# Soft mixture of experts on one core: SP's queue reordered between two products, and the part sums of one weight set begun a stage later

## The chip, the cores and the metric

The kernel runs on one core of one Trainium2 chip. The metric is the device time of one execution in microseconds (us), lower is better; times of several executions are given by their median. The engines are TensorE (PE in the profile, its weight loads PEld), VectorE (DVE), ScalarE (ACT), GpSimd (POOL) and SyncE (SP). SP, ACT and POOL also issue the transfers (DMAs) between the chip's memory and the core.

## The reference

Eight experts, every token goes to all of them, weighted by a softmax over its router logits. Inputs are x (16 x 512 x 512), router_logits (16 x 512 x 8) and expert_weights (8 x 512 x 2048), all float32.

```python
probs = softmax(router_logits)                 # over the 8 experts
output = zeros(16, 512, 2048)
for e in range(8):
    output += probs[:, :, e:e+1] * (x @ expert_weights[e])
```

Written as one product, each token has a row of 8 x 512 entries (x times the probability of each expert), which is multiplied by a matrix of 4096 x 2048.

## The kernel before

The one large product is split as in Strassen's scheme, so that fewer multiplications are needed and sums take their place. On the outermost level there are seven products, P1 to P7, over halves of tokens, experts and columns; each works on a left operand (tokens times probabilities, z tiles, made by VectorE) and a right operand (a sum of weight blocks, w tiles). Every product is done for 16 blocks q of tokens, and inside of it the same scheme is used again: seven inner steps, in the order 1, 5, 6, 2, 7, 3, 4, each of eight matmuls of 512 columns into a PSUM bank. Some stages go a level deeper still.

The work stands in a list of stages. A stage holds one or two products and takes the inner steps of the two in turn, so a stage with two has 14 places, called slots (0 to 13). After a step, its result is copied out of the bank by ScalarE or added by VectorE (the function post). P5 and P6 share stages: k5 = 15 holds P5 of blocks 0 and 1, stage 16 P6 of block 0 alone, stages 17 to 30 hold P6 of block q and P5 of block q + 1, and k6 = 31 holds P6 of block 15. P7 and P4 begin at k7 = 32, and P3 at k3 = 48.

Three things set the order of the work around the steps:

- Hooks. `at(stage, slot, make)` says that make is called ahead of the step in that slot. Loads, fetches of weights and the queueing of sums all hang on such hooks. `slots_after` moves a place on by a number of slots, across stages.
- VectorE's queue. `later(cost, make)` puts a sum into a queue; with a last argument of True at its front. The program takes from it by a plain reckoning of how far TensorE and VectorE are. `flush(task)` takes from it until a given task is done. What comes out of this is a fixed order of instructions for VectorE.
- The queues of SP, ACT and POOL. Each issues its transfers in the order in which the program calls them, and an instruction at the head of a queue waits there for its semaphores. ACT's queue holds both its copies out of the banks and its fetches of weights.

After each step, run(stage) also calls three sets of loads, by n, the number of steps done:

```python
                if n == 5:
                    store_loads(stage + 1)
                if n == 7:
                    finish_loads(stage + 2)
```

finish_loads issues two DMA transposes on SP, which turn a block of x that POOL has loaded and cast (tile xs) into tile xT. store_loads stores the transposed block to memory (x) for later products. Both go through SP's queue.

SP's queue in stages 15 to 31 also carries: the four base fetches of P6 (function fetch_at: the parts of P1 that were kept in memory, h tiles), from which VectorE subtracts P5's results (joined); two stores of each left operand of P6 (keep_z); the loads of x and of the probabilities for the stage after next; and in four places an early part of P3's left operand (the table EARLY: stages k5 + 5, + 8, + 11, + 12). This early part is made in tile u, of which there is a single buffer, by early_make, and stored by SP to operand3.

P4's weights are made from the second half of the weights (loaded anew, block 21) less sums called t2, and from these the inner sums. by_parts does this in four parts, 38 slots apart, each in one w tile:

```python
    by_parts(k5 + 2, 4, 38, 4, load_p4, less_t2, (9, 20))
```

A part loads four blocks by POOL (at the given stage and slot), subtracts t2 from three of them 9 slots later and stores these (less_t2), and queues four inner sums 20 slots after the load, each of which is stored by POOL as soon as it is made (sums_in_place; the DRAM tiles are called wd). w tiles come from a pool of 15 buffers. The first part loads at stage 17, slot 4; the last at stage 25, slot 6, and its sums are queued at stage 26, slot 12.

In stage k6 - 3 = 28, begin_ahead (slot 1) fetches a block of the weights of P7 (t3) into a new w tile, and ahead_part (slots 2 and 13) fetches parts of it into tile u, all on ACT's queue. turnover fetches P4's finished weights from stage k6 on.

Of the kernel before, what the change touches and what calls it, by code (L numbers as in the profile page):

```python
# [31 lines left out]
def kernel(  # L32
# [68 lines left out]
    def note(i):  # L101
        last[i.ins.engine] = i.ins
        if ordered[0]:
            tc.keep_in_program_order(i)
# [18 lines left out]
    def sp(o, i):  # L123
        note(nc.sync.dma_start(out=o, in_=i))

    def pool(o, i, **how):
        note(nc.gpsimd.dma_start(out=o, in_=i, **how))  # L127
# [12 lines left out]
    def new_w():  # L140
        return wpool.tile([P, K8, NB], f16, name="w", tag="w")

    def new_u():
        return zpool.tile([P, K8, HQ], f16, name="u", tag="u", bufs=1)
# [223 lines left out]
    class Task:  # L368
# [5 lines left out]
        def run(self):  # L374
            self.done = True
            clock["dve"] += self.cost
            self.make()

    def flush(task):
        while task is not None and not task.done:  # L380
            queue.popleft().run()
# [6 lines left out]
    def later(cost, make, first=False):  # L388
        t = Task(cost, make)
        (queue.appendleft if first else queue.append)(t)  # L390
        return t
# [9 lines left out]
    def slack(slot=SLOT, lag=LAG, late=None):  # L401
        clock["dve"] = max(clock["dve"], clock["pe"])
        clock["pe"] += slot
        while queue and clock["dve"] < (clock["pe"] - lag if late is None else clock["pe"] + late - queue[0].cost):
            queue.popleft().run()
# [56 lines left out]
    class Left:  # L462
# [11 lines left out]
        def make(self, k):  # L474
            if self.of is not None:
                need(self.of.task[k])
            if self.onto is not None:
                t = self.t[k] = self.onto.half(k)
                u = new_u()
                times(u, k, self.xb, self.pb)  # L480
                tt(t, u, t, SUB)
                return
            t = self.t[k] = new_z()
            times(t, k, self.xb, self.pb)
            if self.less is not None:
                u = new_u()
                times(u, k, *self.less)
                tt(t, t, u, SUB)
            if self.of is not None:
                tt(t, self.of.t[k], t, SUB)  # L490
            if self.kept is not None:
                tt(t, t, self.kept.half(k), SUB)
# [61 lines left out]
    class LoadedLeft(Left):  # L554
# [6 lines left out]
        def load(self, k):  # L561
            self.t[k] = new_z()
            sp(self.t[k], self.sources[k])
# [223 lines left out]
    INNER = ((0, 0), (1, 1), (0, 1), (1, 0))  # L787
# [5 lines left out]
    def at(stage, slot, make):  # L793
        hooks.setdefault((stage, slot), []).append(make)

    def add(*products):
        stages.append(products)
        return len(stages) - 1
# [88 lines left out]
    operand3 = {what: dram.tile([P, K8, HQ], f16, name="operand3") for what in EARLY}  # L887
# [11 lines left out]
    def start_loads(stage):  # L899
        if stage < len(stages):  # L900
            for p in stages[stage]:
                for load in p.loads:
                    if not load.by_hook:
                        load.begin()

    def finish_loads(stage):
        if stage < len(stages):
            for p in stages[stage]:
                for load in p.loads:
                    load.finish()  # L910

    def store_loads(stage):
        if stage < len(stages):
            for p in stages[stage]:
                for load in p.loads:
                    load.store()
# [180 lines left out]
    def queue_lefts(stage):  # L1097
        if stage in thirds:
            if not thirds[stage].task:
                thirds[stage].queue(k7 <= stage < k3)  # L1100
        elif stage < len(stages):
            for p in stages[stage]:
                queue_left(p.left)

    def run(stage):
        some = stages[stage]
        if stage in twos:
            twos[stage].queue()
        for p in some:
            p.left.queue_i()  # L1110
        n = by_thirds(stage) if stage in thirds else by_ones(stage) if stage in ones_ else 0
        if stage in twos:
            n = by_twos(stage)
        for i in range(n // 2, len(some[0].steps)):
            for p in some:
                for make in hooks.get((stage, n), ()):
                    make()
                p.step(p.steps[i])
                slack(late=LATE if len(some) == 2 and 4 <= n < 12 else None)
                p.post(p.steps[i])  # L1120
                n += 1
                if n == wait_for.get(stage, 1):
                    queue_lefts(stage + 1)
                if n == late.get(stage, 1):
                    start_loads(stage + 2)
                if n == 5:
                    store_loads(stage + 1)
                if n == 7:
                    finish_loads(stage + 2)

    def fetch_at(stage, slot, base, *tns):
        for tn in tns:
            at(stage, slot, lambda tn=tn: base.fetch(tn))
# [13 lines left out]
    k5 = add(product(5, 0), product(5, 1))  # L1147
# [3 lines left out]
    k6 = add(product(6, 15))  # L1151
# [18 lines left out]
    def joined(q, tn):  # L1170
        m1 = bases[6, q]
        m1.task[tn] = later(0.69, lambda: tt(m1.t[tn], m1.t[tn], products[5, q].o[tn], SUB), True)

    for q in range(16):
        k = k5 + 1 + q
        duo = len(stages[k - 1]) == 2
        for slot, tn in zip((2, 4, 6, 8) if duo else (1, 2, 3, 4), INNER):
            fetch_at(k - 1, slot, bases[6, q], tn)
        for tn, where in zip(INNER, ((k - 1, 12), (k - 1, 13), (k - 1, 13), (k, 3)) if duo
                             else ((k - 1, 5), (k - 1, 6), (k - 1, 6), (k, 3))):  # L1180
            at(*where, lambda q=q, tn=tn: joined(q, tn))
# [10 lines left out]
    for n, q in enumerate(ORDER_7[1:], 1):  # L1192
        stage = k7 + 2 * n
# [71 lines left out]
    for i, (kn, e) in enumerate((kn, e) for kn in (ODD, (0, 0), (1, 1), (1, 0)) for e in range(2)):  # L1265
        stage = ND + i - 2 if kn != ODD else 2 + 2 * i
# [18 lines left out]
    def sums_in_place(part, b, r, cost):  # L1285

        def one(p, o, x, y):
            def make():
                tt(o, x, y, SUB)
                part(p, o)  # L1290
            return later(cost, make)
        one(5, b[0, 0], b[0, 1], b[0, 0])
        one(7, b[0, 1], b[1, 1], b[0, 1])
        one(6, b[1, 1], b[1, 1], b[0, 0])
        return one(4, b[1, 0], b[1, 0], b[1, 1])
# [13 lines left out]
    def slots_after(stage, slot, n):  # L1309
        slot += n  # L1310
        while slot >= 7 * len(stages[stage]):
            slot -= 7 * len(stages[stage])
            stage += 1
        return stage, slot

    def part_of(what, kn, chunks):
        return kept_w(what, kn)[:, chunks, :]
# [3 lines left out]
    def by_parts(stage, slot, every, r, load, between, when):  # L1321

        for j in range(4):
            b, chunks = {}, ds(2 * j, 2)

            def begin(b=b, j=j, chunks=chunks):
                flush(last_part[0])
                t = new_w()
                for i, kn in enumerate(ORDER):
                    b[kn] = t[:, ds(2 * i, 2), :]  # L1330
                    load(b[kn], kn, j, chunks)

            def go_on(b=b, chunks=chunks):
                for kn in b:
                    if kn != ODD:
                        between(b[kn], kn, chunks)

            def end(b=b, chunks=chunks):
                last_part[0] = sums_in_place(lambda p, o: pool(part_of((r, p), (0, 0), chunks), o), b, r, 0.69)
            at(*slots_after(stage, slot, j * every), begin)  # L1340
            if between is not None:
                at(*slots_after(stage, slot, j * every + when[0]), go_on)
            at(*slots_after(stage, slot, j * every + when[-1]), end)
# [19 lines left out]
            pool(part_of("t4", kn, chunks), t)  # L1363
        later(0.69, make)

    by_parts(k5 + 2, 4, 38, 4, load_p4, less_t2, (9, 20))


    RAW = {1: (0, 0), 2: (1, 0), 3: (1, 1)}
# [89 lines left out]
    def early_make(what):  # L1459
        q, k = what  # L1460
        of = lefts[6, q]
        flush(of.task[k])
        u = new_u()
        times(u, 0, of.xb, early_p[what])
        tt(u, u, of.t[k], SUB)
        sp(operand3[what], u)
    for what, (stage, slot) in EARLY.items():
        at(*slots_after(k5 + stage - 1, slot, 7), lambda what=what: early_begin(what))
        at(k5 + stage, slot, lambda what=what: later(2.45, lambda: early_make(what), True))
    third2, third3 = {}, {}  # L1470

    def third_at(stage, slot, of, r, p):
# [128 lines left out]
    for k in range(len(stages)):  # L1601
        run(k)
# [28 lines left out]
```

## Time and profile before

| | |
|---|---|
| median of 3 runs | 1351.88 us (1351.76 to 1352.21) |
| the profiled execution's own time | 1351.14 us |
| its span | 1349.4 us |
| granted TensorE clock | 1.0 |
| matmuls | 7122 |
| DMA queue of POOL (software) | 176.72 MB, 57.5% of the 16 engines' span |
| DMA queues of SP and ACT (hardware) | 146.15 and 22.15 MB |

The span runs from the first to the last instruction that was recorded; the execution's own time has what lies around it too. A row of the groups or the timeline names the line (often that of a helper: L113 is every VectorE sum, L124 SP's issues, L127 POOL's, L136 every matmul, L170 the fetch of weights on ACT's queue), the engine, the operation, and what it writes and reads by the program's names. Idle time stands behind it with what ended it. In the view of waits, a row has the total, the number of waits and the longest.

### The profile page before, as it was taken

What the parts mean: (1) busy time and instruction counts of PE and PEld (TensorE: products, weight loads), DVE (VectorE), ACT (ScalarE), POOL (GpSimd) and SP (SyncE); (2) the same over time, 40 slices, a digit from 0 to 9 for tenths busy, and PEclk for the clock granted to TensorE, in tenths of its full rate; (3) what the DMA queues carried; (4) which work ended last, traced back from release to release, by engine and by line L of the source; (5) the groups of instructions that cost most, each with busy time, mean ns of one, the idle gap of its engine ahead of it and who ended that gap; (6) DMA issues with size and microseconds to landing.
All of it is one profiled execution on the core that took longest, in us unless ns stands there. A gap on an engine that the chain in (4) does not pass through costs nothing.

```text
span 1349.4 us, 19491 instructions
## 1 busy us (share of the span) xinstructions
PE 1343.5 (100%) x7122; PEld 693.1 (51%) x7122; DVE 1166.6 (86%) x1483; ACT 281.8 (21%) x593; POOL 403.9 (30%) x619
## 2 busy tenths in 40 slices
PE   9999999999999999999999999999999999999998
PEld 4465655565544444444444444554555455556564
DVE  7888898989989889797897889889898989898984
ACT  3333423223211111111111100110111111224331
POOL 3223322333323232323312112424333231232342
PEclk9999999999999999999999999999999999999999
DMA  9999979999899999999998789999999989999997
GB/s 182 249 216 239 262 247 235 299 292 281 248 320 293 310 290 294 289 320 262 318 320 263 297 314 186 241 244 217 238 248 229 217 220 306 303 185 232 263 161 133
DMA packets 185392, 346.26 MB, mean 257 GB/s; under 512 B 52176, under 2 KB 81616, under 8 KB 181200
## 3 DMA queue, kind: packets, MB, share of 16 engines
q0 software_dynamic: 84960, 176.72, 57.5%
q1 hardware_dynamic: 97024, 146.15, 35.8%
q10 hardware_dynamic: 3312, 22.15, 4.4%
q8 instruction: 55, 0.90, 0.3%
q14 instruction: 41, 0.34, 0.1%
HBM read 203.19 MB, written 174.26 MB: 280 GB/s over the span
## 4 chain that ended last, share of the span: by engine, by line
PE 99%; DMA 1%; POOL 0%; issue 0%; ACT 0%; POOLq 0%
PE ps L136 78%; PE pt L136 21%; DMA w<-in_expert_weights_dram 1%; POOL w L127 0%; ACT h L1568 0%; POOL ident L234 0%; POOLq L234 0%; POOLq L1615 0%
## 5 line engine op out<-in xcount | busy, mean ns | idle before, releaser
L136 PE MATMUL ps<-w,z 128*128 128x512 f16 (+1 forms) x3884 | 840.1, 372 | 0.0
L136 PEld LDWEIGHTS <-z 128*128 128x128 f16 x5236 | 511.7, 98 | 538.1 <-issue 0.3
L127 POOL DMA_DIRECT2D out_dram<-h x380 | 251.8, 679 | 726.2 <-ACT h L751 323.2
L113 DVE TENSOR_TENSOR h<-ps,h 128x512 f32<-128x512 f32 x318 | 214.6, 684 | 59.2 <-PE ps L136 58.1
L136 PE MATMUL pt<-w,z 128*128 128x512 f16 (+1 forms) x1304 | 253.2, 338 | 0.2 <-DMA w<-in_expert_weights_dram 0.2
L113 DVE TENSOR_TENSOR z<-xT,pT 128x2048 f16<-128x2048 f16 x188 | 226.5, 1216 | 2.2 <-DMA xT<-xs 2.2
L136 PE MATMUL ps<-w,d 128*128 128x512 f16 x880 | 200.7, 379 | 0.0
L738 ACT COPY h<-ps 128x512 f32<-128x512 f32 x102 | 59.7, 585 | 394.0 <-PE ps L136 394.0
L136 PEld LDWEIGHTS <-d 128*128 128x128 f16 x880 | 86.0, 98 | 96.5
L113 DVE TENSOR_TENSOR z<-z,d 128x2048 f16<-128x2048 f16 x110 | 131.7, 1216 | 0.0
L113 DVE TENSOR_TENSOR w<-w 128x1024 f16<-128x1024 f16 (+2 forms) x106 | 116.0, 1113 | 2.6 <-PE ps L136 1.0
L113 DVE TENSOR_TENSOR d<-z 128x1024 f16<-128x1024 f16 x110 | 74.0, 684 | 1.0
L113 DVE TENSOR_TENSOR h<-pt,h 128x512 f32<-128x512 f32 x75 | 51.3, 686 | 27.0 <-PE pt L136 22.8
L751 ACT COPY h<-ps 128x512 f32<-128x512 f32 x54 | 31.6, 586 | 203.8 <-PE ps L136 167.6
L113 DVE TENSOR_TENSOR ps<-ps,h 128x256 f32<-128x256 f32 (+1 forms) x84 | 50.6, 603 | 21.0 <-PE ps L136 15.1
L734 ACT COPY h<-ps 128x512 f32<-128x512 f32 x89 | 49.9, 599 | 69.9 <-PE ps L136 64.2
L127 POOL DMA_DIRECT2D kept<-h x56 | 30.6, 547 | 87.0 <-DVE h L113 49.7
L113 DVE TENSOR_TENSOR z<-z 128x2048 f16<-128x2048 f16 (+1 forms) x52 | 50.5, 977 | 1.5
L730 ACT COPY ps<-ps 128x512 f32<-128x512 f32 x47 | 26.8, 570 | 107.4 <-PE ps L136 71.1
L113 DVE TENSOR_TENSOR h<-h 128x512 f32<-128x512 f32 (+2 forms) x69 | 45.0, 674 | 0.1
L127 POOL DMA_DIRECT2D out_dram<-kept x40 | 42.1, 1152 | 0.2 <-issue 0.2
L136 PEld LDWEIGHTS <-h 128*128 128x128 f16 x384 | 37.5, 98 | 4.4
(109 smaller groups left out, 690.8 us busy)
## 6 DMA issues: line engine op xcount, KB each, us to landing
out_dram<-h POOLq DMA_DIRECT2D x380, 256.0 KB, 7.3
z<-z SPq DMA_DIRECT2D x56, 512.0 KB, 8.4
pT<-p_dram SPq DMA_DIRECT2D x93, 256.0 KB, 7.7
h<-kept SPq DMA_DIRECT2D x88, 256.0 KB, 6.2
w<-wd ACTq DMA_DIRECT2D x20, 1024.0 KB, 8.7
w<-in_expert_weights_dram POOLq DMA_DIRECT2D x33, 512.0 KB, 12.1
xT<-x SPq DMA_DIRECT2D x63, 256.0 KB, 7.2
h<-out_dram SPq DMA_DIRECT2D x60, 256.0 KB, 8.8
```

The costliest lines, as they stand in the source:

```text
L113: dve(nc.vector.tensor_tensor(out=o, in0=a, in1=b, op=op))
L127: note(nc.gpsimd.dma_start(out=o, in_=i, **how))
L136: note(nc.tensor.matmul(ps, z, w, start=start, stop=stop, skip_group_check=True))
L730: act(nc.scalar.copy(self.banks["b"], x))
L734: act(nc.scalar.copy(o[tn], q if p == 5 else x))
L738: act(nc.scalar.copy(o[TN[p]], b if p == 2 else x))
L751: act(nc.scalar.copy(o[tn], b))
```

## The change

Four groups of edits, all on what runs beside the matmuls; the matmuls and their order are the same.

1. In stages from k5 up to, not including, k6 that hold two products, the stores of x (store_loads) come after 11 steps and no longer after 5, and the transposes (finish_loads) after 8 and no longer after 7.
2. The fourth base fetch of P6 hangs on slot 7, before on slot 8.
3. The early part of P3's left operand is made where it was, but its store on SP's queue is no longer called when VectorE's task is taken; it hangs on a hook of its own, five slots after the task was queued, and takes the task from the queue if that has not been done yet.
4. by_parts for P4's weights begins at stage k5 + 3, before at k5 + 2; everything in it moves by a stage.

The last part is now loaded at stage 26, slot 6, and its sums are queued at stage 27, slot 12.

```diff
-                if n == 5:
+                kept_amid = k5 <= stage < k6 and len(some) == 2
+                if n == (11 if kept_amid else 5):
                     store_loads(stage + 1)
-                if n == 7:
+                if n == (8 if kept_amid else 7):
                     finish_loads(stage + 2)
...
-        for slot, tn in zip((2, 4, 6, 8) if duo else (1, 2, 3, 4), INNER):
+        for slot, tn in zip((2, 4, 6, 7) if duo else (1, 2, 3, 4), INNER):
             fetch_at(k - 1, slot, bases[6, q], tn)
...
-    by_parts(k5 + 2, 4, 38, 4, load_p4, less_t2, (9, 20))
+    by_parts(k5 + 3, 4, 38, 4, load_p4, less_t2, (9, 20))
...
         tt(u, u, of.t[k], SUB)
-        sp(operand3[what], u)
+        early_u[what] = u
+
+    def early_store(what):
+        flush(early_task[what])
+        sp(operand3[what], early_u[what])
+    early_u, early_task = {}, {}
+
+    def early_queue(what):
+        early_task[what] = later(2.45, lambda: early_make(what), True)
     for what, (stage, slot) in EARLY.items():
         at(*slots_after(k5 + stage - 1, slot, 7), lambda what=what: early_begin(what))
-        at(k5 + stage, slot, lambda what=what: later(2.45, lambda: early_make(what), True))
+        at(k5 + stage, slot, lambda what=what: early_queue(what))
+        at(*slots_after(k5 + stage, slot, 5), lambda what=what: early_store(what))
```

## The prediction

> **What bounds the kernel now.** I read the page's busy times and its chain first, then what TensorE (PE) waited for, then TensorE's own rows. The page:
>
> ```profile
> PE 1343.5 (100%) x7122; PEld 693.1 (51%) x7122; DVE 1166.6 (86%) x1483; ACT 281.8 (21%) x593; POOL 403.9 (30%) x619
> ...
> PE 99%; DMA 1%; POOL 0%; issue 0%; ACT 0%; POOLq 0%
> ```
>
> The view of waits, TensorE alone; then its timeline at the start (start, duration, line, operation, count) and its groups with shapes kept apart (busy us, mean ns of one):
>
> ```profile
> PE every L95 <- DVE h L92: 1.3, 1, 1.3
> PE ps L136 <- DMA w<-in_x_dram: 0.4, 1, 0.4
> PE ps L136 <- DVE lg L304: 0.3, 1, 0.3
> PE pt L136 <- DMA w<-in_expert_weights_dram: 0.2, 1, 0.2
> ...
> 1.29 4.45 PE L95 MATMUL every<-h 128*128 128x512 f16 x10 [1.29 <-DVE h L92]
> ...
> 24.11 4.05 PE L136 MATMUL ps<-w,z 128*128 128x512 f16 x18
> ...
> L136 PE MATMUL ps<-w,z 128*128 128x512 f16 x3624 | 801.8, 379 | 0.0
> ...
> L95 PE MATMUL every<-h 128*128 128x512 f16 x10 | 4.4, 632 | 1.3 <-DVE h L92 1.3
> ```
>
> Four waits, 2.2 us in all, all in the first ten microseconds. A busy TensorE need not be a TensorE at its rate, so I take the pace: 18 matmuls in 4.05 us, of which the last one alone lasts 0.38 (the group's 379 ns), so (4.05 - 0.38) / 17 = 0.216 us from start to start. Stretches far from there keep it: further down, 16 matmuls take 3.62 us, and (3.62 - 0.38) / 15 is 0.216 again. Eight of them, 1.73 us, I call a slot; 14 slots are a stage with two products. TensorE is therefore the bound from one end to the other with no hole for an edit to fill. The order of its 14,246 rows in the built program is the same before and after. An edit of queues and of VectorE (DVE) order can then gain nothing beyond the 2.2 us at the start, which it doesn't touch. The question is only whether it opens a hole, and where.
>
> **The part sums, one stage later.** The last of the four parts decides, since what comes behind it stays where it was. Stage 27 starts near 669.6 and stage 28 near 693.8 us: the first ACT copy of P5's first bank ends a stage's second slot, and it comes at 673.30 and 697.48, 24.18 us apart. Timelines of DVE, POOL, ACT and PE around there, with the tile view of the four stores between:
>
> ```profile
> 669.88 1.41 DVE L113 TENSOR_TENSOR w<-w 128x1024 f16<-128x1024 f16 x2
> ...
> 672.13 1.41 DVE L113 TENSOR_TENSOR w<-w 128x1024 f16<-128x1024 f16 x2
> ...
> 671.25 1.18 POOL L127 DMA_DIRECT2D wd<-w  x2
> 672.50 0.71 POOL L127 DMA_DIRECT2D xs<-in_x_dram  x1
> 673.48 0.56 POOL L127 DMA_DIRECT2D wd<-w  x1 [0.27 <-issue]
> 674.83 0.54 POOL L127 DMA_DIRECT2D wd<-w  x1 [0.79 <-DVE z L113]
> ...
> L127 POOL DMA_DIRECT2D wd<-w x4: 540/540/557, 671.2 to 674.8; - x4
> ...
> DMA to landing us min/median/max: 6.5/7.0/7.2
> ...
> 673.30 0.57 ACT L730 COPY ps<-ps 128x512 f32<-128x512 f32 x1 [2.88 <-PE ps L136]
> ...
> L170 ACTq DMA_DIRECT2D w<-wd x1: 326/326/326, 694.1 to 694.1; - x1
> ...
> 694.13 0.33 ACTq L170 DMA_DIRECT2D w<-wd  x1
> 697.48 0.57 ACT L730 COPY ps<-ps 128x512 f32<-128x512 f32 x1 [2.92 <-DMA out_dram<-h]
> 697.58 0.33 ACTq L1389 DMA_DIRECT2D u<-wd  x1
> ...
> 697.22 3.62 PE L136 MATMUL pt<-w,z 128*128 128x512 f16 x16
> 700.67 3.62 PE L136 MATMUL ps<-w,d 128*128 128x512 f16 x16
> ```
>
> Four sums, four stores; the last store is issued at 674.83 and has landed 6.5 to 7.2 us later, at 681.3 to 682.0. At 694.13 ACT issues the fetch of the t3 weights (the function begin_ahead, stage k6-3 = 28, slot 1). It is the only weight fetch into a w tile on ACT's queue from 420 to 720 us (the tile view of that stretch, the row w<-wd x1). What it waits for can be read in the built program's order with its waits: in the kernel before on DMASW4, 3, 1 and 0, in the changed one on DMASW4, 2, 5 and 1, in each case the semaphores of exactly these four stores. It gets the buffer of the part tile. Today the stores have landed 12 us ahead of it. One stage later they land at 681.7 (the middle) + 24.18 = 705.9, some 11.8 us after the fetch wants to go. The DVE rows in the changed program stand in the same place of stage 28 as these do of stage 27 (behind the join sums, around P6's first base sum), so I move them by the whole stage, with POOL's cast of x between them as before.
>
> Behind the waiting fetch on ACT's queue stands the copy of L730, which moves P5's first result out of its bank. TensorE waits for this copy with the slot that adds product 6 into that bank: the second half of the row at 700.67, so from 700.67 + 1.73 = 702.40. Today the copy ends at 697.48 + 0.57 = 698.05, which leaves 4.35 us; that is all the cover there is. Afterwards: landing 705.86, issue of the fetch 0.33, copy 0.57, and up to 0.1 from the copy's end to the matmul (the copy at 697.48 began 0.1 after the end, 697.22 - 0.216 + 0.38, of the matmul that it waited for), so 706.8; the hole is 706.8 - 702.4 = 4.4 us. Everything after it on TensorE shifts by this, as no later hole takes it back; DVE and POOL gain slack from it.
>
> No row shows the new landing itself. The nearest are the other parts' four stores (tile view, the three earlier parts):
>
> ```profile
> DMA to landing us min/median/max: 8.3/8.8/9.3
> ...
> DMA to landing us min/median/max: 6.7/8.5/10.1
> ...
> DMA to landing us min/median/max: 3.3/6.2/8.0
> ```
>
> With 3.3 us the last store lands at 674.83 + 24.18 + 3.3 = 702.3 and the hole is 0.8 us; with 10.1 it is 7.6. I keep the middle of the last part's own pair, 6.85, since the neighbours on POOL and DVE are the same ones; 0.8 and 7.6 stay as ends. Nothing below zero: TensorE has no idle time there to lose. The other three parts move with no fetch of ACT behind them, and keep their tiles' readers on DVE and POOL, so I cost them at nothing; their tiles' next takers are the parts themselves, which still come 38 slots apart.
>
> **SP's order.** Four edits in a stage: the store of the early operand leaves VectorE's place in the order and goes five slots later; the store of x goes from slot 5 to slot 11; the transposes go from 7 to 8; the fourth base fetch from slot 8 to 7, so ahead of the transposes. The views: SP's waits, the timeline of stage 27, the tile view of u.
>
> ```profile
> SPq L432 <- DMA xs<-in_x_dram: 114.3, 18, 17.8
> ...
> SPq L124 <- DVE u L113: 23.7, 4, 7.3
> ...
> 678.09 0.32 SPq L124 DMA_DIRECT2D operand<-u  x1
> 678.50 0.38 SPq L124 DMA_DIRECT2D h<-kept  x1
> 678.93 0.77 SPq L124 DMA_DIRECT2D x<-xT  x1
> ...
> 680.90 3.25 SPq L432 DMA_TRANSPOSE xT<-xs  x2
> 684.20 0.98 SPq L124 DMA_DIRECT2D h<-kept  x1
> ...
> DMA to landing us min/median/max: 3.1/6.2/9.0
> ```
>
> The edits take a wait for u of up to 7.3 us out of the way of the base fetches, and bring the fourth fetch (684.20) ahead of the transposes. Neither pays: the base sums are DVE's, and TensorE did not wait for them. What moves back: the early store by five slots and the transposes at most, 678.09 + 8.6 + 3.25 = 689.9, landed by 693 to 699. Its tile u has one buffer, and the next taker is ACT's fetch at 697.58, which the hole above moves to 706.8 anyway: covered. Without that cover, 1.4 us more on ACT's queue, still inside the copy's 4.35. The store of x is six slots, 10.4 us, later, in tiles of which five are taken in a stage and ten exist: a stage of cover. The transposes, 1.73 us later, feed products that are made a stage after. All four at nothing.
>
> **The sum.** The profiled execution took 1351.14 us (span 1349.4 and 1.7 around it): 1351.14 + 4.4 = 1355.5. The runs' median, 1351.88, is 0.74 above it, and I forecast it in the same way: 1351.88 + 4.4 = 1356.3, slower by 0.33%. A measurement of this kernel tells about 0.2%, 2.7 us, from no change.
>
> **The rivals.**
>
> The clock falls in the hole. The rows at the top show that TensorE starts slow after idleness: ten matmuls in 4.45 us, one of them lasting 0.63, so (4.45 - 0.63) / 9 = 0.424 us each against 0.216, so ten of them lose 2.1 us. If a hole of 4.4 us brings that back, the time is 1356.3 + 2.1 = 1358.4. For it: the hole is as long as the slow stretch itself. Against it: the slow rows at the start follow an engine that had not run at all, not four microseconds of rest, and nothing in mid-kernel shows such a rest. The Trainium skill, "TensorE: Matmul & The Clock Gate", Part 1, has a rule for it: one idle window of about 3.4 us halves the clock, until one busy window lifts it, and the windows run free of the program. The opening rows agree in factor and length; by that rule a hole of this size halves the clock in some runs and in others not. Chance 0.24.
>
> Not slower (the other side). The fetch still waits, but the stores land early, as in the third part: the hole closes with a landing under about 2.5 us and is under 2.7 us with one under 5.2 (0.8 at 3.3, and a microsecond for each). Time 1351.9 to 1354.5. For it: the row 3.3/6.2/8.0, and ACT's fetches not yet on the DMA engines while it waits. Against it: what decides is the last of four stores, and the four parts' slowest took 9.3, 10.1, 8.0 and 7.2. Also here: that the copy could pass the waiting fetch, which no row shows. Chance 0.10.
>
> SP becomes the wait. If the base fetches or the stores of x, now behind the transposes' wait for their cast (17.8 us at longest), come too late in several stages, VectorE's sums are late and TensorE with them. Point from which it decides: a delay past the stage of cover. One such place of the same depth as the hole, 4.4 us, gives 1360.7. Against it: the fetches move forward, not back. Chance 0.05.
>
> That the change does nothing of what it says is excluded by the built order: the four stores stand one stage later on POOL.
>
> **How the numbers follow.** Forecast 0.60; cold clock 0.24; not slower 0.10; SP 0.05; faster 0.01, for an unknown. The low end is set at a hole of 2.5 us, 1354.4; the high end at a hole of 6.4 with the cold clock, 1351.9 + 6.4 + 2.1 = 1360.4. Left out are the rival below, 0.10, and the ends above, some 0.07. Faster by over 0.2%: 0.01; within: 0.10; slower: 0.89.
>
> **What would show it.** In the profile after: one wait of TensorE near 702 us, at L136 on ACT's copy L730, of 3 to 7 us, and no other; the fetch on ACT's queue not at 694 but near 706, straight behind the landing of a wd store; no wait of ACT on u; after the hole, matmuls at 0.216 us, or some ten at 0.42 if the clock fell. Wrong would be: TensorE without a hole, or the hole elsewhere, above all with a DVE sum or an h fetched by SP as its releaser.

## The result, and the profile after

The changed kernel takes 1362.05 us (median of 6 runs, 1360.98 to 1362.35) against 1351.82 (6 runs, 1351.27 to 1353.29): 1.007 times as long, 95% interval 1.0057 to 1.0083. It is slower by 10.2 us, where 4.4 was forecast, and above the range.

The page of the profile after, busy times and chain, then TensorE's waits:

```profile
PE 1344.6 (99%) x7122; PEld 694.0 (51%) x7122; DVE 1167.2 (86%) x1483; ACT 282.3 (21%) x593; POOL 404.9 (30%) x619
...
PE 91%; issue 4%; DMA 3%; POOL 1%; DVE 1%; ACT 0%; POOLq 0%; ACTq 0%; DVEq 0%
...
PE ps L136 <- ACT ps L730: 8.5, 1, 8.5
PE every L95 <- DVE h L92: 1.3, 1, 1.3
PE ps L136 <- DMA w<-in_x_dram: 1.2, 2, 0.7
PE pt L136 <- DMA w<-in_expert_weights_dram: 0.4, 1, 0.4
PE ps L136 <- DVE lg L304: 0.3, 1, 0.3
```

One wait is new, and it is the forecast one: TensorE on ACT's copy L730. The chain, which was TensorE from end to end, now leaves it for a store of the part sums (wd). The timelines of stage 28, DVE, POOL, ACT and PE, with the tile view of the four stores:

```profile
694.33 1.41 DVE L113 TENSOR_TENSOR w<-w 128x1024 f16<-128x1024 f16 x2
696.58 1.41 DVE L113 TENSOR_TENSOR w<-w 128x1024 f16<-128x1024 f16 x2
...
695.66 1.07 POOL L127 DMA_DIRECT2D wd<-w  x2
696.76 0.72 POOL L127 DMA_DIRECT2D xs<-in_x_dram  x1
697.57 0.56 POOL L127 DMA_DIRECT2D wd<-w  x1
698.47 0.54 POOL L127 DMA_DIRECT2D wd<-w  x1 [0.34 <-issue]
...
DMA to landing us min/median/max: 9.5/11.0/11.6
...
710.28 0.33 ACTq L170 DMA_DIRECT2D w<-wd  x1
710.70 0.57 ACT L730 COPY ps<-ps 128x512 f32<-128x512 f32 x1 [15.87 <-DMA wd<-w]
...
700.96 1.89 PE L136 MATMUL ps<-w,d 128*128 128x512 f16 x8
711.33 3.33 PE L136 MATMUL ps<-w,d 128*128 128x512 f16 x8 [8.48 <-ACT ps L730]
```

The sums and the stores stand one stage (24.1 to 24.5 us) behind their places of before, the last store 23.6. But the stores land 9.5 to 11.6 us after their issue, not 6.5 to 7.2. The last lands at 698.47 + 11.64 = 710.11 (the chain has this piece, below), the fetch goes at 710.28, the copy ends at 711.27, and TensorE, which would have gone on at 700.96 + 8 x 0.216 = 702.69, goes on at 711.33: a hole of 8.64 us. The eight matmuls behind it take 3.33 us where eight took 1.89 just before. The view by windows shows why (length, then PE, PEld, DVE, ACT and POOL busy, granted clock, DMA share, GB/s):

```profile
700.00:702.40 2.40, 2.40 (x13) 1.08 (x11) 2.40 (x4) 0.00 (x0) 0.00 (x0) 1.00 1.13 171
702.40:711.30 8.90, 0.45 (x3) 0.10 (x1) 8.34 (x9) 0.60 (x2) 0.00 (x0) 0.78 0.84 216
711.30:715.00 3.70, 3.67 (x11) 1.39 (x11) 0.00 (x0) 0.80 (x2) 0.00 (x0) 0.60 0.90 328
```

The granted clock is 1.00 ahead of the hole, falls inside it and is still 0.60 on average in the 3.7 us behind it. So the profiled execution's 1361.74 - 1351.14 = 10.6 us are 8.64 of hole, 1.44 of slow matmuls, 0.28 of a later start behind the first loads (the row of 24.11 now stands at 24.39), and 0.2 of a short stop near 1102, which the runs with the later fetch, with slot 0 and with slot 1 have too, near 1092.

### The profile page after: what moved, and what is told of

The parts are those of the page before. It is cut to its first block, busy times and chain, and to the rows that moved or that the text cites. A ratio compares the mean times of both kernels' runs of the same rounds, so it can differ in the third digit from the quotient of the medians.

```text
span 1360.0 us, 19504 instructions
## 1 busy us (share of the span) xinstructions
PE 1344.6 (99%) x7122; PEld 694.0 (51%) x7122; DVE 1167.2 (86%) x1483; ACT 282.3 (21%) x593; POOL 404.9 (30%) x619
## 4 chain that ended last, share of the span: by engine, by line
PE 91%; issue 4%; DMA 3%; POOL 1%; DVE 1%; ACT 0%; POOLq 0%; ACTq 0%; DVEq 0%
PE ps L136 72%; PE pt L136 19%; DMA wd<-w 2%; POOL out_dram L127 1%; DMA w<-in_expert_weights_dram 1%; DVE z L113 0%; POOL wd L127 0%; POOL w L127 0%; POOL xs L127 0%; DVE h L113 0%; DVE d L113 0%; DVE w L113 0%; ACT ps L730 0%; POOLq L127 0%; DVE ps L113 0%
## 5 line engine op out<-in xcount | busy, mean ns | idle before, releaser
L730 ACT COPY ps<-ps 128x512 f32<-128x512 f32 x47 | 26.8, 571 | 120.3 <-PE ps L136 71.0
```

Source lines behind the costliest of these rows:

```text
L730: act(nc.scalar.copy(self.banks["b"], x))
```

## The experiments

Ten kernels were run, with four or ten executions each, beside executions of the kernel before. The baseline's median was 1351.66 us beside the first four, 1351.56 beside the next four, 1351.90 beside the last two.

**The part sums alone.** The kernel before with one edit:

```diff
-    by_parts(k5 + 2, 4, 38, 4, load_p4, less_t2, (9, 20))
+    by_parts(k5 + 3, 4, 38, 4, load_p4, less_t2, (9, 20))
```

> The kernel before with the part sums one stage later and nothing else; SP's order is that of before. Theory A (the four SP edits filled the transfer queues ahead of the last stores, which is why they landed after 11.6 us and not after 6.85): the last store lands after about 7 us, the hole at the matmul that waits for L730 is about 4.4 us, the time 1351.9 + 4.4 = 1356.3, or 1358 if the clock falls. Theory B (stage 28 is fuller than stage 27 by itself, since in stage 27 SP stood for 7 us and let the queues drain; SP's edits are not needed): landing after 11 to 12 us, hole 8 to 9 us, eight slow matmuls, time 1361.5 to 1362.5.

1362.18 us, ratio 1.0077 (1.0062 to 1.0092). TensorE's wait, and the stores' landing:

```profile
PE ps L136 <- ACT ps L730: 8.4, 1, 8.4
...
DMA to landing us min/median/max: 10.1/10.6/10.8
...
700.06 10.49 DMA wd<-w
```

The last line is the last store's piece of the chain: it lands after 10.49 us. The whole loss is there without any edit of SP's order. Theory A falls: the late landing needs no edit of SP.

**SP's order alone.** The changed kernel with by_parts back at k5 + 2.

> The changed kernel with the part sums where they were before, so the SP edits alone. Theories A and B both: no wait of TensorE after the first ten microseconds, no slow matmuls, 1351.9 within 0.7 us; the SP edits cost nothing by themselves. Rival C (the SP edits make a hole of their own somewhere in stages 15 to 31): 1354 or more, with a wait of TensorE on a DVE sum.

1351.78 us, ratio 1.0003 (0.9994 to 1.0012); TensorE waits only in the first ten microseconds. Rival C falls. The run also shows something else. Here the four stores stand in stage 27, as before, but SP no longer stands (waits at the head of its queue) there for the early operand, and issues transfers in the time in which it stood. The stores' landing goes from 6.5/7.0/7.2, with 6.5 for the last one, to the following, with 9.3 for the last one:

```profile
DMA to landing us min/median/max: 6.6/8.2/9.3
```

**The fetch later, the parts late as in the change.**

```diff
-    at(k6 - 3, 1, begin_ahead)
-    for e, load, go in ((0, (k6 - 3, 2), (k6 - 3, 9)), (1, (k6 - 3, 13), (k6 - 2, 6))):
+    at(k6 - 3, 9, begin_ahead)
+    for e, load, go in ((0, (k6 - 3, 2), (k6 - 2, 3)), (1, (k6 - 2, 7), (k6 - 1, 0))):
```

> The changed kernel, whole, but the fetch of the t3 block stands eight slots later on ACT's queue (stage 28, slot 9 and not 1), behind the copies of that stage; its parts and their two sums follow it later too. The part sums are still one stage later and their stores still land near 710. If the hole comes from the copy L730 standing behind the waiting fetch (theories A and B): no hole, no slow matmuls, 1351.9 within 0.7 us. If the late part sums cost something by themselves, in DVE's order or by their stores (rival D): 1354 or more with the hole at another place.

1351.67 us, ratio 0.9999 (0.9989 to 1.0008). ACT's timeline:

```profile
697.84 0.57 ACT L730 COPY ps<-ps 128x512 f32<-128x512 f32 x1 [2.92 <-PE ps L136]
...
711.65 0.34 ACTq L170 DMA_DIRECT2D w<-wd  x1
```

The fetch goes even later than in the changed kernel (711.65 against 710.28), yet nothing is lost, since the copy stands ahead of it. This shows the mechanism: here late part sums cost nothing by themselves, and the copy queued behind the fetch that waits for their stores is the whole loss. Rival D falls.

**Smaller shifts.** The changed kernel with the parts beginning at slot 0, 1, 2 and 3 of stage k5 + 3 in place of 4.

> The changed kernel, but the part sums begin four slots (6.9 us) earlier, at stage k5 + 3, slot 0. The fetch waits for the same kind of stores. With landings as late as in the changed kernel, 710.1 - 6.9 = 703.2, the copy is late by 8.6 - 6.9 = 1.7 us: a hole of 0 to 2 us at the same place, and no slow matmul if a hole needs some length to slow the clock; 1351.9 to 1354. If the hole doesn't go with the landing of the stores: 1360 or more.

> The changed kernel with the part sums at stage k5 + 3, slot 1, three slots earlier than in the changed kernel and one later than in the run with slot 0, where the fetch waited to 698.46 and the copy ended 1.9 us later than before, with no hole. The last store one slot later lands near 700 to 704: no hole, or one under 2.5 us and no slow matmul; 1351.7 to 1354.5.

> The same with slot 2. In the built order of VectorE, the last of the four sums falls behind the next product half, so its store is made some 5 us later than with slot 1. If the hole goes with the last store's landing: 3 to 7 us. If the slow clock needs a hole of about the length of the slow stretch at the start, 3 to 4 us, this run shows it or not by its size: with it 1.6 us more. 1355 to 1361.

> The same with slot 3, one slot short of the changed kernel. Last sum and store within a microsecond of the changed kernel's by the built order, so a hole of 6 to 9 us with about eight slow matmuls, 1358.5 to 1362.

The times were 1351.83 (ratio 1.0001, 0.9992 to 1.0011), 1352.04 (0.9999, 0.9987 to 1.0010), 1358.22 (1.0049, 1.0034 to 1.0064) and 1359.68 (1.0060, 1.0045 to 1.0075). ACT's fetch in the four, and TensorE's wait in the last two:

```profile
698.46 0.33 ACTq L170 DMA_DIRECT2D w<-wd  x1
...
700.49 0.33 ACTq L170 DMA_DIRECT2D w<-wd  x1
...
705.67 0.34 ACTq L170 DMA_DIRECT2D w<-wd  x1
PE ps L136 <- ACT ps L730: 3.8, 1, 3.8
...
708.09 0.34 ACTq L170 DMA_DIRECT2D w<-wd  x1
PE ps L136 <- ACT ps L730: 5.0, 1, 5.0
```

At 700.49 there is no hole, at 705.67 one of 4.00 us, at 708.09 one of 5.1, less than the 6 to 9 that were expected for slot 3. The hole follows the fetch one for one: in the slot-2 run 705.67 - 4.00 = 701.67, in the changed kernel 710.28 - 8.64 = 701.64 is the moment from which it costs. In the slot-3 run it is 708.09 - 5.12 = 702.97, as all of stage 28 stands 1.3 us later in that profile, by its first loads. The hole is not proportional to the slots: VectorE's order moves the last sum by a whole product half between slots 1 and 2, so that the last store is issued at 692.74 with slot 1 and at 697.62 with slot 2; the landings, 7.6 to 8.6 us after the last store's issue, do the rest. The slot-0 run had no hole where up to 2 us were allowed for, since its last store landed at 698.4 and not at 703.

**SP made to stand.** The parts alone, and SP stands on the last part sum, as it stands in stage 27 on the early operand; the edit's main lines:

```diff
...
+                def part(p, o):
+                    pool(part_of((r, p), (0, 0), chunks), o)
+                    if j == 3 and p == 4:
+                        sp(stand, o[:, 0, 0:16])
```

> The part sums one stage later on SP's old order (as in the run of the parts alone), with one thing added that is not in the computation: SP stores 16 columns of the last sum, 4 KB, to a scratch tensor, and stands in its queue until this sum is made, with one base fetch ahead of it and the next base fetch, a store of x and a store of z behind it, much as SP stands in stage 27 for the early operand. Theory B1 (the last stores landed late since SP, which doesn't stand in stage 28, puts its transfers of 0.26 to 0.52 MB in ahead of them): the last store lands after 7 to 8 us, the hole is 4.4 to 5.5 us, the time 1356.3 to 1357.5, and with a slower clock 1358 to 1359. Theory B2 (the queues are full in stage 28 from what was issued before, whatever SP does): landing after 10 to 12 us, hole over 7 us, 1360.5 to 1362.5.

1360.31 us, ratio 1.0065 (1.0050 to 1.0080), with a hole of 6.04 us. Landing, SP's row that ended the stand and the next one, and TensorE behind the hole:

```profile
DMA to landing us min/median/max: 7.3/8.2/8.7
...
698.19 0.32 SPq L124 DMA_DIRECT2D stand<-w  x1
698.68 0.34 SPq L124 DMA_DIRECT2D h<-kept  x1
...
708.90 3.57 PE L136 MATMUL ps<-w,d 128*128 128x512 f16 x8 [5.88 <-ACT ps L730]
```

The last store now lands after 8.7 us, where 10.5 was measured with the parts alone. The time lies between the ranges of B1 and B2: transfers that SP issues ahead of the last store are a part of the lateness. The stand is not as long as that of stage 27. It ended at 698.19, 0.7 us ahead of the last store's issue at 698.87, while in stage 27 SP stood until 678.09, 3.3 us past that issue; so SP's next transfers ran beside the last store here.

**SP made to stand longer.** The parts alone, and SP stands on P6's step 5 in stage 28; the edit's main line:

```diff
...
+    at(k6 - 3, 3, lambda: sp(stand, products[6, 12].o[1, 1][:, 0:16]))
```

> The run of the parts alone with SP standing longer: at stage 28, slot 3, SP stores 16 columns of P6's result of step 5, 8 KB, to a scratch tensor (not in the computation), and so stands until about 700.7, two microseconds past the issue of the last part store; in the run before, the stand ended 0.7 us ahead of it. Theory B1 (SP's transfers explain the late landing): the last store lands after 7 to 8 us, the hole is 4.4 to 5.3 us, and with about 1.7 us of slow clock 1357.7 to 1358.8. Theory B3 (SP explains only the part that the shorter stand took away; the rest is what POOL itself queued): landing after 8.5 to 9.5 us as with the shorter stand, 1359.5 to 1361.

1360.47 us, ratio 1.0056 (1.0039 to 1.0073); hole 7.0 us. Landing of the four, the last store's piece of the chain, and SP's rows from the stand on:

```profile
DMA to landing us min/median/max: 8.5/8.6/9.5
...
699.88 8.70 DMA wd<-w
...
700.26 0.32 SPq L124 DMA_DIRECT2D stand<-h  x1
700.75 0.34 SPq L124 DMA_DIRECT2D h<-kept  x1
...
702.16 0.38 SPq L124 DMA_DIRECT2D h<-kept  x1
```

The longer stand takes nothing more off; the last store again lands after 8.7 us, as B3 expected. So 1.8 us of the lateness go with the transfers that SP issues ahead of the last store, and 2.2 us against the 6.5 of stage 27 remain. B3's reason for these, a longer queue of POOL's own, is not shown, and the traces speak against it: when the last store is issued, POOL has the same seven transfers out in this run and in the kernel before (three of out_dram, three of wd, one of xs). The other candidates are the transfers behind the stand. The last store was issued 1.2 us later than meant, so the stand ended 0.4 us past its issue and not two; SP's next four transfers, issued from 700.75 on, ran beside the store, which was out to 708.58. In stage 27 SP issues nothing for 3.3 us past the issue. No run held SP that long in stage 28, so the cause of the 2.2 us stays open.

**The fetch one slot later.** As the run with the later fetch, but with begin_ahead at (k6 - 3, 2), just behind the copy L730.

> As the run with the later fetch, but the fetch of the t3 block stands at stage 28, slot 2: one slot later than in the changed kernel, just behind the copy L730, with the two copies of L734 behind it. The stores land near 710 to 711.5 as before. L730 is free, so there is no hole at 702. The next copy that TensorE needs early is the second of L734 (P5's step 6, out of the bank into which step 7 adds from slot 9, near 709.4). Landing 710.1 to 711.5, fetch 0.33, two copies of 0.59: a hole of 2 to 3.7 us there, by my theory that ACT's queue holds back what stands behind the fetch. If a hole needs 3.4 us or so to slow the clock, a hole under 3.4 shows no slow matmul: 1353.7 to 1355.3. If any hole slows it, 1.6 us more.

1353.32 us, ratio 1.0008 (0.9999 to 1.0018). ACT's and TensorE's timelines and the clock:

```profile
698.38 0.57 ACT L730 COPY ps<-ps 128x512 f32<-128x512 f32 x1 [2.92 <-PE ps L136]
710.66 0.33 ACTq L170 DMA_DIRECT2D w<-wd  x1
...
712.05 0.59 ACT L734 COPY h<-ps 128x512 f32<-128x512 f32 x1
...
705.03 5.34 PE L136 MATMUL ps<-w,z 128*128 128x512 f16 x24
712.70 1.89 PE L136 MATMUL ps<-w,z 128*128 128x512 f16 x8 [2.32 <-ACT h L734]
...
709.00:713.00 4.00, 1.68 (x9) 0.69 (x8) 3.03 (x4) 1.43 (x3) 0.00 (x0) 1.00 0.53 113
```

The hole has moved to the next copy that TensorE needs, as expected: 712.70 - (705.03 + 24 x 0.216) = 2.5 us. The eight matmuls behind it take 1.89 us, full speed, and the clock stays 1.00. The profiled execution, 1354.56 us, is the slowest of ten; their median lies 1.4 us above the baseline's and 0.4 below the expected range, so the hole may have been shorter in most of them. The interval of the ratio just takes in no difference; the hole itself is in the trace.

## Why the prediction was wrong

- That nothing could be gained, as TensorE had no hole: right. No kernel here beats the one before.
- The place and the chain of causes (late sums, late stores, a fetch at the head of ACT's queue that waits for the part's buffer, the copy L730 behind it, the bank of P5's step 6): right at each link. The chain after carries them in this order, start, length and what:

```profile
698.47 11.64 DMA wd<-w
...
710.28 0.33 ACTq L170
...
710.70 0.58 ACT ps L730
```

- The step that failed is the landing of the last store. The prediction kept "the middle of the last part's own pair, 6.85, since the neighbours on POOL and DVE are the same ones". They were; SP was not the same. In the rows that the prediction itself quoted, SP stood in stage 27 until 678.09, when it could store the early operand, and had a base fetch, a store of x and one of z behind that. The prediction read this stand only as a wait in the way of the base fetches. The stores of the parts were issued to 674.83, so they had the queues without those. Stage 28 has no early operand. SP's rows up to the last store, the kernel before (its next issue is the one at 678.09), then the parts alone (last store at 700.06):

```profile
670.41 0.32 SPq L124 DMA_DIRECT2D h<-kept  x1
...
689.50 3.54 SPq L124 DMA_DIRECT2D h<-kept  x2
693.15 1.01 SPq L124 DMA_DIRECT2D x<-xT  x1
694.21 1.27 SPq L124 DMA_DIRECT2D z<-z  x1
700.58 0.32 SPq L124 DMA_DIRECT2D h<-kept  x1
```

  The SP edits, which take the stand in stage 27 away, put 2.8 us on the last store (6.5 to 9.3, SP's order alone); putting a stand into stage 28 takes 1.8 off it (10.5 to 8.7). Why the rest of the lateness is there, 2.2 us with the parts alone, stays open. With 11.64 in place of 6.85 the landing adds 4.8 us to the hole, and the earlier issue of the last store takes 0.5 off: 4.4 + 4.8 - 0.5 = 8.7, against 8.64 measured. The upper end, 7.6, rested on 10.1 us, the slowest of the other parts, and was too low as well; the range itself ended at a hole of 6.4 with 2.1 of slow clock.
- The clock was taken as a rival with a chance of 0.24, at 2.1 us. It fell in every profile with a hole of 4.0 us or more, six kernels, and cost 1.4 to 2.0 us. The size was nearly right, but the term belonged into the sum: a hole shorter than the forecast's own 4.4, of 4.0 us, had it too. The rule of the Trainium skill, "TensorE: Matmul & The Clock Gate", Part 1, that an idle window of about 3.4 us halves the clock, agrees with these runs as far as the length goes: no slow matmul behind 2.5 us, slow ones behind 4.0. The prediction read it as a matter of luck at this length, and no run here tells how often a hole of 2.5 to 4.0 us has it. A window that is idle throughout is not what the slot-2 run shows: the 3.4 us ahead of the clock's fall, 703.9 to 707.3, held 0.6 us of matmuls.
- SP's four edits at nothing: right for the time (1.0003, 0.9994 to 1.0012), and no wait of TensorE came from the tile u. But they are not nothing for the transfers beside them, as the landing of 9.3 shows.

## What to carry to other kernels

When a step is moved, the waits behind it are found by following its buffers to their next taker, and what counts is what stands behind that taker on its own queue. A transfer's landing time belongs to the place where it is issued, not to the transfer (here 6.5 us in stage 27, 10.5 to 11.6 for the same store in stage 28): before moving one, look at what every issuing queue does at the new place, those too that stand still at the old one. In this kernel, whose TensorE has no other holes, each hole of four microseconds or more cost 1.4 to 2.0 us beyond its length, as the clock fell with it; and a fetch put behind the copies of its stage instead of ahead of them cost nothing here with the same late stores.

## What the runs showed of the hardware

The clock's fall needs a length: none behind a hole of 2.5 us, and behind 4.0, 5.1, 6.0, 7.0, 8.5 and 8.6 us each time seven to ten matmuls at half speed, so 1.4 to 2.0 us whatever the length, one profile for each length. By the clock's records in the traces the fall came 3.4 to 4.8 us after the hole began, so in the longer holes a part of the slow time passed while TensorE stood anyway. In the run with slot 2 the fall even came when the hole was over. TensorE resumed at 706.73; the view by windows has the clock at 1.00 ahead, then falling:

```profile
704.00:706.00 2.00, 0.00 (x0) 0.00 (x0) 1.97 (x3) 0.00 (x0) 0.00 (x0) 1.00 1.02 401
706.00:708.00 2.00, 1.27 (x5) 0.59 (x5) 2.00 (x2) 1.12 (x2) 0.00 (x0) 0.83 1.50 263
708.00:710.00 2.00, 2.00 (x7) 0.63 (x5) 1.86 (x3) 0.21 (x1) 0.00 (x0) 0.50 0.95 343
```

The same 256 KB stores of the last part landed 5.3 to 12.9 us after their issue on POOL in these runs (5.3 with slot 1, 12.9 with the later fetch); with the later fetch TensorE had no hole, and none of this was to be seen in the time.
